# Channel mixer of layer 1 over all tokens at once, in seven block products instead of eight

## The chip, the cores and the metric

The kernel runs on one core of a Trainium2 chip. The metric is the device time of one execution in microseconds. TensorE (PE) multiplies, VectorE (DVE) and GpSimd (POOL) do elementwise work, ScalarE (ACT) casts and activations, SyncE (SP) issues the transfers between DRAM and the core's memory (SBUF). Products are accumulated in PSUM.

## What is computed

A trunk of two layers over 1024 tokens of width 1024. Each layer has a token mixer (RWKV in the first, sparse attention, DSA, in the second) and a channel mixer; shift, scale and gate of each come from a projection of a conditioning vector. The channel mixer has a hidden width of 2816:

```python
def _swiglu(h, w_in, w_out):
    gate, up = jnp.split(h @ w_in, 2, axis=-1)
    return (jax.nn.silu(gate) * up) @ w_out
...
        x = _layernorm(DEEPNORM_ALPHA * x + (1 + gt1) * y, ln_g[i, 0], ln_b[i, 0])
        hin = x * (1 + sc2) + sh2
        y = _swiglu(hin, ffn_w_in[i], ffn_w_out[i])
        x = _layernorm(DEEPNORM_ALPHA * x + (1 + gt2) * y, ln_g[i, 1], ln_b[i, 1])
```

## The kernel before

Every large product is made of three products of rounded parts: each operand is split into a high part (`whi`, a cast on ACT, L204) and a low part (`wlo`, the difference, on DVE or POOL in a rota kept in `low`, L121), and `mm3` (L232 to 235) multiplies high by high, high by low and low by high. One matmul is 128 rows of weights by 512 columns, `128x512` in the profile.

`ffn(0, (0, 1), zt, rest, x=x)` is the channel mixer of the first layer. It takes the tokens in two halves of 512. For each half and each of 22 column blocks `j` of 128, `gate_up` makes the gate (24 matmuls) and the up product (24 matmuls), the silu, the product of the two (L1171, DVE) and its high and low parts (`hid`). The down product follows after groups of 8, 7 and 7 blocks (`FG`), and `evac_y` (L812, L813) adds it into the residual rows `R`. Those were scaled by the previous LayerNorm's gain and bias in `resid` (L806, L807, on POOL, 128x1024). At the end come the LayerNorms (`layernorm`, L818 to L832), which write `z` back to DRAM (L829).

Other work is threaded into it. The tail of the token mixer runs step by step from the generator `bg`, four steps for each call of `rest`; its last parts are two output pairs of 48 matmuls (`psg<-whi,oq`), their LayerNorm and the write of the second half's rows. `ada_v(1, ·)` makes twelve columns of the next layer's modulation: four loads of 512 KB, eight operations on DVE (L305, L307) and four small matmuls (L310) each. `hin_prep` transposes `z` (L886) and makes the next hidden input with its parts (L890 to L892), for the second half of this mixer and for the next layer while PE goes on with products. The engines take their instructions in the order in which a scheduler placed them; a load goes out on SP when its buffer is free. Weights come through three buffers `wst` of 128x1024, the modulation through buffers `z` of a pool `big`.

## Time and profile before

| | before |
|---|---|
| median of 3 runs | 3320.2 us (3309.88 to 3321.77) |
| the profiled execution | 3313.66 us, span 3311.9 us, mean granted clock 0.958 |
| PE busy, share of the span | 3066.4 us, 93% |
| DVE | 2154.5 us, 65% |
| ACT | 1351.4 us, 41% |
| POOL | 993.9 us, 30% |
| DRAM traffic | 438.42 MB, mean 132 GB/s |
| the stage of this mixer | 1018.9 to 1809.8 us |

Busy shares are of the whole span, and stages differ; the views of the next but one section are therefore cut to the stage. A busy PE is one with a matmul in flight: the pipelined matmuls overlap, so the time from one to the next, and not the duration of one, is its price. The granted clock (PEclk) is 1.00 at 2.4 GHz and 0.50 at 1.2 GHz.

### The profile page before, as it was taken

The page shows a single profiled execution, that of the slowest core. Times are in us where ns is not written, and L with a number is a line of the kernel's source. Part 1 is how long each engine was busy: PE and PEld are TensorE (multiplying, and loading weights), DVE is VectorE, ACT ScalarE, POOL GpSimd, SP SyncE. Part 2 cuts the span into 40 slices and gives each one's busy share as a digit, 9 for nine tenths or more (in the row PEclk, how much of TensorE's full clock was granted, in tenths as well). Part 3 has the DMA queues.
Part 4 walks back from the last instruction along what each step waited for, and adds up shares of the span by engine and source line. Part 5 has one row for each costly group of instructions (what it writes and reads, how often), then busy time and mean ns, then how long its engine had stood idle before and what let it go on. Part 6 is the DMA issues. An engine that isn't in the chain of part 4 may idle for free. (4 is left out here: it accounts for less than half of the span.)

```text
span 3311.9 us, 48942 instructions
## 1 busy us (share of the span) xinstructions
PE 3066.4 (93%) x17888; PEld 2414.2 (73%) x17888; DVE 2154.5 (65%) x4239; ACT 1351.4 (41%) x2512; POOL 993.9 (30%) x780
## 2 busy tenths in 40 slices
PE   6889689989989999999999999988999999899998
PEld 2466257688777788877888776677887777687886
DVE  4576578756766764583334577786697788775345
ACT  3552344234444222232223745646622466452223
POOL 3261135201112411251112122556222432443112
PEclk8989888999999999999999999998999999999999
DMA  6556756598874653463332622244323411253333
GB/s 195 145 167 175 131 173 171 138 180 156 187 171 123 229 188 115 154 224 102 93 99 94 186 83 73 65 132 139 96 90 111 143 63 34 91 167 101 92 99 121
DMA packets 611057, 438.42 MB, mean 132 GB/s; under 512 B 207936, under 2 KB 508480, under 8 KB 610816
## 3 DMA queue, kind: packets, MB, share of 16 engines
q1 hardware_dynamic: 610816, 435.29, 47.0%
q8 instruction: 141, 2.31, 0.3%
q14 instruction: 100, 0.82, 0.1%
HBM read 379.12 MB, written 55.95 MB: 131 GB/s over the span
## 5 line engine op out<-in xcount | busy, mean ns | idle before, releaser
L204 ACT CAST whi<-wst 128x512 fp32r<-128x512 f32 x886 | 541.4, 619 | 1262.0 <-PE psu L234 569.7
L121 POOL TENSOR_TENSOR wlo<-wst,whi 128x512 fp32r<-128x512 f32 x330 | 460.7, 1397 | 1508.8 <-ACT whi L204 1474.8
L121 DVE TENSOR_TENSOR wlo<-wst,whi 128x512 fp32r<-128x512 f32 (+1 forms) x556 | 470.8, 851 | 504.2 <-ACT whi L204 498.7
L233 PE MATMUL psu<-hin,whi 128*128 128x512 f32 (+1 forms) x1568 | 587.5, 375 | 39.2 <-DVE sl L1171 22.4
L234 PE MATMUL psu<-hin,whi 128*128 128x512 f32 (+1 forms) x1568 | 586.6, 374 | 8.4 <-DVE hin L907 3.3
L235 PE MATMUL psu<-hin,wlo 128*128 128x512 f32 (+1 forms) x1568 | 584.5, 373 | 0.1
L233 PEld LDWEIGHTS psu<-hin,whi 128*128 128x128 f32 x1568 | 301.9, 193 | 93.7 <-DVE sl L1171 25.6
L234 PEld LDWEIGHTS psu<-hin,whi 128*128 128x128 f32 x1568 | 302.6, 193 | 60.2 <-DVE hin L907 6.1
L235 PEld LDWEIGHTS psu<-hin,wlo 128*128 128x128 f32 x1568 | 302.1, 193 | 50.6 <-POOL wlo L121 0.6
L234 PE MATMUL psg<-wlo,hid 128*128 128x512 f32 x528 | 206.4, 391 | 0.0
L233 PE MATMUL psg<-whi,hid 128*128 128x512 f32 x528 | 205.2, 391 | 0.0
L235 PE MATMUL psg<-whi,hid 128*128 128x512 f32 x528 | 205.1, 389 | 0.0
L233 PE MATMUL psg<-xs,whi 128*128 128x512 f32 x384 | 164.1, 436 | 19.8 <-ACT whi L204 11.0
L234 PE MATMUL psg<-xs,whi 128*128 128x512 f32 x384 | 164.9, 430 | 8.4 <-POOL xs L121 5.7
L235 PE MATMUL psg<-xs,wlo 128*128 128x512 f32 x384 | 161.2, 421 | 1.7 <-DVE wlo L121 1.7
L1171 DVE TENSOR_TENSOR sl<-sl,psu 128x512 f32<-128x512 f32 (+1 forms) x98 | 61.7, 630 | 148.3 <-PE psu L235 138.2
L233 PEld LDWEIGHTS psg<-xs,whi 128*128 128x128 f32 x384 | 77.8, 204 | 52.5 <-ACT whi L204 13.0
L233 PEld LDWEIGHTS psg<-whi,hid 128*128 128x128 f32 x528 | 99.1, 188 | 20.9
L235 PEld LDWEIGHTS psg<-whi,hid 128*128 128x128 f32 x528 | 99.1, 188 | 20.8
L234 PEld LDWEIGHTS psg<-wlo,hid 128*128 128x128 f32 x528 | 99.2, 188 | 20.8 <-DVE wlo L121 0.6
L115 ACT ACTIVATE z<-z,mx 128x128 f32<-128x128 f32 (+7 forms) x128 | 99.2, 776 | 32.6 <-DVE mx L1529 31.6
L234 PEld LDWEIGHTS psg<-xs,whi 128*128 128x128 f32 x384 | 77.2, 201 | 38.3 <-issue 9.7
(418 smaller groups left out, 6472.2 us busy)
## 6 DMA issues: line engine op xcount, KB each, us to landing
wst<-in_ffn_w_in_dram SPq DMA_DIRECT2D x196, 512.0 KB
wst<-in_ffn_w_out_dram SPq DMA_DIRECT2D x92, 512.0 KB
wst<-in_rwkv_w_rkv_dram SPq DMA_DIRECT2D x48, 512.0 KB
z<-in_ada_w_dram SPq DMA_DIRECT2D x48, 512.0 KB
wst<-in_ada_w_dram SPq DMA_DIRECT2D x32, 512.0 KB
wst<-in_rwkv_w_out_dram SPq DMA_DIRECT2D x64, 256.0 KB
wst<-in_dsa_w_out_dram SPq DMA_DIRECT2D x32, 512.0 KB
wst<-in_dsa_w_in_dram SPq DMA_DIRECT2D x26, 512.0 KB
```

The source lines that it names most:

```text
L115: return A.activation(o, i, f, **kw)
L121: i = eng.tensor_tensor(lo, x, hi.bitcast(F32), op=OP.subtract)
L204: A.copy(h_[:, :m], st[:, c:c + m])
L233: mm(o, lh, rh, start=first, stop=False)
L234: mm(o, lh, rl, start=False, stop=False)
L235: mm(o, ll, rh, start=False, stop=last)
L1171: V.tensor_tensor(sl[:, c], sl[:, c], ou[:, c], op=OP.mult)
```

## The change

`ffn` is no longer used for this mixer; `ffn_both(0, x)` takes its place. Tokens, inner width and outer width are each cut in two, and both products are made of seven block products instead of eight, after Strassen and Winograd: sums and differences of the blocks of the operands are multiplied, and the results are added to each other.

- **Up.** For each column block `j` seven products of 12 matmuls (`prod`), with four combinations of the four weight blocks (`b11`, `b12`, `b21`, `b22`; half the inner width, gate or up) on DVE and POOL. The combinations of the hidden input (`s2`, `s3`, `s1`, `a22`, `s4`, high and low, 40 tiles) are made once, from `z` read back from DRAM through `wst` and transposed (L1311 of the changed kernel). They need both halves of the tokens; so the products of four blocks (`NP = 4`) with the first half alone are made ahead, under the tail of the token mixer, and kept in the `R` buffers. The results are joined by additions from PSUM on DVE, silu and product follow (`gmul`, POOL), and of each pair of blocks `j` and `j + 11` the hidden blocks and their combinations, seven in all, go to `hd` in DRAM.
- **Down.** The 22 blocks of the down weights are loaded whole, 44 loads of 256 KB, and stay; their memory is that of the combinations of the hidden input. Each product reads its seven times 11 hidden blocks back from `hd` through `wst` and splits them (cast on ACT, low on DVE); the combinations of the weights `t1` to `t4` are made on DVE and POOL, and all lows of weights are POOL's. The residual rows are scaled by DVE and POOL in turn, four rows each.
- **Moved.** `ada_v` uses `wst` instead of `big`, two columns each at `jj = 2` and `4` and one each at the even `jj` from 6 to 20. The pool `big` is opened after the mixer, three small factor tiles are freed ahead of it. The hidden input of the mixer's second half is no longer made by `hin_prep`, and that of the next layer comes after the last product.

The program of PE has 15025 instructions before and 14661 after, 396 matmuls of 128x512 fewer and 32 transposes more.

```diff
+    fp_ = pool(sf, "fac")
...
     sc0.close()
+    sf.close()
     sb.close()
...
-                bp.append(pool(ctx, "big", side="right"))
...
-    ffn(0, (0, 1), zt, rest, x=x)
+    def prod(o, w, c, xh, xl, first):
+        (h_,), (l_,) = w
+        for k in range(4):
...
+            mm(o, h_[:, s], xh[k][:, c], start=first and k == 0, stop=False, **kw_)
+            mm(o, h_[:, s], xl[k][:, c], start=False, stop=False, **kw_)
+            mm(o, l_[:, s], xh[k][:, c], start=False, stop=k == 3, **kw_)
...
+    def ffn_both(l, x):
...
+        hd = tc.dram_tile([7, FP, P, HN], F32, name=f"hd{l}")
...
+            ws2 = lambda: f.tile([P, 1024], F32, tag="ws2", bufs=2, name="ws2")
...
+            def wload(t, off):
+                dma(t.rearrange("p (k n) -> p k n", n=P), dap(win, bi + off, [[2 * FH, P], [P * 2 * FH, KT], [1, P]]))
+                return t[:, 0:HN], t[:, HN:2 * HN]
...
+            (a11h, a12h), (a11l, a12l) = ((t[0:4], t[4:8]) for t in x)
...
+            for j in range(0, NP, 2):
...
+                for i in range(2):
+                    b11, b21 = wload(wst(), (j + i) * P)
+                    kept.append(rtile())
...
+                    prod(o[i], split(b11, HN), full, a11h, a11l, True)
+                    A.copy(kept[-1][:, 0:HN], o[i])
+                    rest(None)
+                for i in range(2):
+                    prod(o[i], split(b2[i], HN), full, a12h, a12l, False)
+                    act(kept[j + i][:, HN:2 * HN], o[i], AF.Silu)
+                    rest(None)
+            while bg:
+                rest(None)
+            with ExitStack() as sc_:
...
+                for nm in ("s2", "s3", "s1", "a22", "s4"):
+                    com[nm] = [[cpool.tile([P, HN], F32R, name=f"{nm}{hl}{i}") for i in range(4)] for hl in "hl"]
+                for i in range(4):
...
+                    for m in range(2):
+                        zb = wst()
+                        for e in range(2):
+                            dma(zb[:, e * HN:e * HN + HN].rearrange("p (a n) -> p a n", n=P),
+                                dap(zd[2 * l][m], (i + 4 * e) * P, [[D, P], [P * D, NTT], [1, P]]))
+                        for e in range(2):
+                            pt = pst()
+                            for b in range(NTT):
+                                nc.tensor.transpose(pt[:, b * P:b * P + P], zb[:, e * HN + b * P:e * HN + b * P + P], ident)
...
+                            act(r_, pt, scale=hsc[:, 2 * l + 1, ft:ft + 1], bias=hbi[:, 2 * l + 1, ft:ft + 1])
+                            raw[m, e] = r_
+                    s1, s2 = hf32(), hf32()
+                    tt(V, s1, raw[1, 0], raw[1, 1], add_)
+                    tt(V, s2, s1, raw[0, 0], sub_)
+                    tt(G, raw[0, 0], raw[0, 0], raw[1, 0], sub_)
+                    tt(V, raw[0, 1], raw[0, 1], s2, sub_)
+                    for n_, (nm, r_) in enumerate((("s2", s2), ("s3", raw[0, 0]), ("s1", s1), ("a22", raw[1, 1]), ("s4", raw[0, 1]))):
...
+                        A.copy(hi_, r_)
+                        sub(G if n_ in (1, 3) else V, lo_, r_, hi_)
...
+                for jj in range(FT):
+                    j = jj // 2 + FP * (jj % 2)
+                    b11, b21 = wload(wst(), j * P)
+                    b12, b22 = wload(ws2(), FH + j * P)
+                    early = j < NP
+                    if early:
+                        u2, sl0 = kept[j][:, 0:HN], kept[j][:, HN:2 * HN]
+                    else:
+                        u2, sl0 = tl("u2", 2), tl("sl0")
+                        oa = psx("u")
+                        prod(oa, split(b11, HN), full, a11h, a11l, True)
+                        A.copy(u2, oa)
+                    tt(V, b11, b12, b11, sub_)
...
+                    tt(V, t2, b22, b11, sub_)
...
+                    prod(ob, split(t2, HN), full, *com["s2"], True)
+                    if not early:
+                        prod(oa, split(b21, HN), full, a12h, a12l, False)
+                        act(sl0, oa, AF.Silu)
+                    tt(V, u2, ob, u2, add_)
+                    tt(G, b12, b22, b12, sub_)
...
+                    prod(oc, split(b12, HN), full, *com["s3"], True)
...
+                    tt(V, u3, oc, u2, add_)
...
+                    prod(od, split(b11, HN), full, *com["s1"], True)
+                    tt(G, b21, b21, t2, sub_)
+                    prod(oc, split(b21, HN), full, *com["a22"], False)
+                    tt(V, u3, od, u3, add_)
...
+                    tt(V, sl1, oc, u2, add_)
+                    act(sl1, sl1, AF.Silu)
...
+                    gmul(h1, u3, sl1)
+                    prod(od, split(b22, HN), full, *com["s4"], False)
+                    tt(V, u2, od, u2, add_)
...
+                    gmul(h0, u2, sl0)
+                    hids[j] = h0, h1
+                    if j >= FP:
+                        (a21, a11), (a22, a12) = hids.pop(j - FP), hids.pop(j)
+                        k = j - FP
+                        for q, t in ((0, a11), (1, a12), (2, a22)):
+                            dma(hd[q, k], t)
+                        s1, s2 = hf32(), hf32()
+                        tt(G, s1, a21, a22, add_)
+                        dma(hd[3, k], s1)
+                        tt(G, s2, s1, a11, sub_)
+                        dma(hd[4, k], s2)
+                        s4 = hf32()
+                        tt(V, s4, a12, s2, sub_)
+                        dma(hd[6, k], s4)
+                        s3 = hf32()
+                        tt(V, s3, a11, a21, sub_)
+                        dma(hd[5, k], s3)
+                    elif l == 0 and nada[0] < 12 and j >= 1:
+                        for _ in range(2 if nada[0] < 4 else 1):
+                            ada_v(1, nada[0], wst, hf32)
+                            nada[0] += 1
...
+            w = [wq.tile([P, D], F32, name=f"wo{k}") for k in range(FT)]
+            for k, n in [(k, 0) for k in range(FT)] + [(k + h * FP, 1) for k in range(FP) for h in (1, 0)]:
+                dma(w[k][:, n * HN:n * HN + HN], dap(wo, bo_ + k * P * D + n * HN, [[D, P], [1, HN]]))
...
+            lg = tp.tile([P, D], F32, name="lg")
+            rmore = [tp.tile([P, D], F32, name=f"Rm{i}") for i in range(NTT)]
...
+            dma(g_, dap(modd[l], (24 + 16) * P, [[0, P], [1, D]]))
...
+            dma(lg, dap(a["ln_g"], i * D, [[0, P], [1, D]]))
+            dma(lbs, dap(a["ln_b"], i * D, [[0, P], [1, D]]))
+            V.tensor_scalar(lg, lg, ALPHA, None, op0=OP.mult)
+            V.tensor_scalar(lbs, lbs, ALPHA, None, op0=OP.mult)
+            rr = [[rtile() for _ in range(NTT)], rmore]
+            for m in (1, 0):
+                for t_ in range(NTT):
+                    r = rr[m][t_]
+                    dma(r, zd[i][m][t_ * P:t_ * P + P, :])
+                    (G if t_ % 2 else V).tensor_tensor(r, r, lg, op=OP.mult)
+                    (G if t_ % 2 else V).tensor_tensor(r, r, lbs, op=OP.add)
+            def t1(k):
+                tt(V, left(k), right(k), left(k), sub_)
+            def t2(k):
+                t1(k)
+                t = f32()
+                tt(G, t, right(k + FP), left(k), sub_)
+                return t
+            def t3(k):
+                tt(G, right(k), right(k + FP), right(k), sub_)
+                return right(k)
+            def t4(k):
+                t = f32()
+                tt(V, t, left(k + FP), right(k + FP), sub_)
+                tt(G, t, t, left(k), add_)
+                return t
+            def product(q, wk, o, first):
+                for k in range(FP):
+                    if k % 2 == 0:
+                        nk = min(2, FP - k)
+                        st_ = wst()
+                        dma(st_[:, :nk * HN].rearrange("p (k n) -> p k n", n=HN), hd[q, k:k + nk].rearrange("k p n -> p k n"))
+                    raw = st_[:, k % 2 * HN:k % 2 * HN + HN]
+                    xh, xl = hint(), hint()
+                    A.copy(xh, raw)
+                    sub(low[0], xl, raw, xh)
...
+                    (wh,), (wl,) = split(wk(k), HN)
+                    for b in range(NTT):
...
+            def out(m, n, o, u):
+                for b in range(NTT):
+                    t = hf32()
...
+                    if u is None:
+                        V.scalar_tensor_tensor(t, gn, 1.0, o[b], op0=OP.add, op1=OP.mult)
+                    else:
+                        tt(V, u[b], o[b], u[b], add_)
+                        V.scalar_tensor_tensor(t, gn, 1.0, u[b], op0=OP.add, op1=OP.mult)
+                    r = rr[m][b][:, n * HN:n * HN + HN]
+                    tt(G, r, r, t, add_)
+            oa, ob = quad(), [psu(), psu(), pst(), pst()]
+            product(0, left, oa, True)
...
+            for b in range(NTT):
+                A.copy(u2[b], oa[b])
+            product(4, t2, ob, True)
+            for b in range(NTT):
+                tt(V, u2[b], ob[b], u2[b], add_)
+            product(1, lambda k: left(k + FP), oa, False)
+            out(1, 0, oa, None)
+            product(5, t3, ob, True)
...
+            for b in range(NTT):
+                tt(V, u3[b], ob[b], u2[b], add_)
+            product(3, left, oa, True)
+            out(0, 1, oa, u3)
+            product(2, t4, ob, False)
+            for b in range(NTT):
+                t = hf32()
+                tt(V, t, ob[b], u2[b], add_)
+                V.scalar_tensor_tensor(t, g_[:, 0:HN], 1.0, t, op0=OP.add, op1=OP.mult)
+                r = rr[0][b][:, 0:HN]
+                tt(V, r, r, t, add_)
+                layernorm(l, 1, 0, b, rr[0][b], tp)
+            product(6, lambda k: right(k + FP), oa, False)
+            out(1, 1, oa, u2)
+            for b in range(NTT):
+                layernorm(l, 1, 1, b, rr[1][b], tp)
+        low[:] = [V, V, G]
+    NP = 4
+    ffn_both(0, x)
+    bp.append(pool(ctx, "big", side="right"))
```

Three places in the order of the instructions, with the names of the programs (a number behind a name tells buffers apart). The first is the end of the token mixer's tail on PE. Before, up products follow the last output pair to the end of the half:

```order
L233 MATMUL psg<-whi,oq 128x512
L234 MATMUL psg<-wlo,oq 128x512
L235 MATMUL psg<-whi,oq 128x512
L233 MATMUL psu<-hin,whi 128x512
L234 MATMUL psu<-hin,whi 128x512
L235 MATMUL psu<-hin,wlo 128x512
```

After, 57 matmuls of the early blocks follow it, and then this; `pst<-cst,wst` are the transposes of the hidden input, `s2`, `s3` its combinations:

```order
L1250 MATMUL psu<-hin,whi 128x512
L1251 MATMUL psu<-hin,whi 128x512
L1252 MATMUL psu<-hin,wlo 128x512
L1311 MATMUL pst<-cst,wst 128x128 x56
L1250 MATMUL psu<-s2h_10271,whi 128x512
L1251 MATMUL psu<-s2l_10275,whi 128x512
L1250 MATMUL psg<-s3h_10279,whi 128x512
L1251 MATMUL psg<-s3l_10283,whi 128x512
L1252 MATMUL psu<-s2h_10271,wlo 128x512
```

Behind the early products stand 56 transposes in one run, and the next product takes a combination of both halves.

The second is a modulation column on DVE. Before, its eight operations (L305, L307) lie among the lows of weights and the gate products of two blocks:

```order
L1171 TENSOR_TENSOR sl<-sl,psu 128x512
L121 TENSOR_TENSOR wlo<-wst,whi 128x512
L311 TENSOR_TENSOR modf<-pst,vf 128x4
L125 TENSOR_SCALAR hid<-sl 128x512
L305 TENSOR_SCALAR yt<-z_12508,csr 128x512
L121 TENSOR_TENSOR hid<-sl,hid 128x512
L307 SCALAR_TENSOR_TENSOR yt<-z_12508,csr,yt 128x512
L307 SCALAR_TENSOR_TENSOR yt<-z_12512,csr,yt 128x512 x2
L307 SCALAR_TENSOR_TENSOR yt<-z_12516,csr,yt 128x512 x2
L121 TENSOR_TENSOR wlo<-wst,whi 128x512
L307 SCALAR_TENSOR_TENSOR yt<-z_12520,csr,yt 128x512 x2
```

After, at `jj = 2`; `hf` is the accumulator, `L1266` the combinations and additions:

```order
L1266 TENSOR_TENSOR sl_10851<-psg,R 128x512
L307 SCALAR_TENSOR_TENSOR hf_10875<-wst,csr,hf_10875 128x512 x3
L1266 TENSOR_TENSOR R<-psg,R 128x512
L307 SCALAR_TENSOR_TENSOR hf_10875<-wst,csr,hf_10875 128x512 x4
L305 TENSOR_SCALAR hf_10898<-wst,csr 128x512
L307 SCALAR_TENSOR_TENSOR hf_10898<-wst,csr,hf_10898 128x512
L311 TENSOR_TENSOR modf<-pst,vf 128x4
L307 SCALAR_TENSOR_TENSOR hf_10898<-wst,csr,hf_10898 128x512 x6
L1266 TENSOR_TENSOR wst<-ws_11079,wst 128x512
L1266 TENSOR_TENSOR wst<-ws_10923,wst 128x512
L311 TENSOR_TENSOR modf<-pst,vf 128x4
L1266 TENSOR_TENSOR t_10946<-ws_10923,wst 128x512
```

The operations of two columns now stand in two long runs, and the combinations of the next block's weights (`wst<-ws,wst`) behind them.

The third is the scaling of the residual rows. Before, on POOL (L806, L807), between lows of weights:

```order
L121 TENSOR_TENSOR wlo<-wst,whi 128x512
L806 TENSOR_TENSOR R<-R,z_13713 128x1024 x2
L807 TENSOR_TENSOR R<-R,z_13714 128x1024
L121 TENSOR_TENSOR wlo<-wst,whi 128x512
L807 TENSOR_TENSOR R<-R,z_13714 128x1024
L806 TENSOR_TENSOR R<-R,z_13713 128x1024
L121 TENSOR_TENSOR wlo<-wst,whi 128x512
L807 TENSOR_TENSOR R<-R,z_13714 128x1024
L806 TENSOR_TENSOR R<-R,z_13713 128x1024
L807 TENSOR_TENSOR R<-R,z_13714 128x1024
```

After, on POOL between product 0 and product 4 of the down product; `L1266` with `hin` makes `t2`, `L121` its low part:

```order
L1266 TENSOR_TENSOR wo_13935<-wo_13946,wo_13935 128x512
L1417 TENSOR_TENSOR R<-R,lg 128x1024 x2
L1417 TENSOR_TENSOR Rm_13993<-Rm_13993,lg 128x1024
L1418 TENSOR_TENSOR R<-R,wst 128x1024 x2
L1417 TENSOR_TENSOR Rm_13995<-Rm_13995,lg 128x1024
L1418 TENSOR_TENSOR Rm_13993<-Rm_13993,wst 128x1024
L1266 TENSOR_TENSOR hin<-wo_13936,wo_13925 128x512
L1266 TENSOR_TENSOR hin<-wo_13937,wo_13926 128x512
L1266 TENSOR_TENSOR hin<-wo_13938,wo_13927 128x512
L1266 TENSOR_TENSOR hin<-wo_13939,wo_13928 128x512
L1418 TENSOR_TENSOR Rm_13995<-Rm_13995,wst 128x1024
L121 TENSOR_TENSOR wlo<-hin,whi 128x512 x4
```

The eight rows' scaling, of which POOL and DVE have half each, stands ahead of the combinations of the second product's weights. On SP the transfers that it needs stand behind the loads of all down weights:

```order
L1398 DMA wo_13934<-in_ffn_w_out_dram 128x512
L1398 DMA wo_13946<-in_ffn_w_out_dram 128x512
L1398 DMA wo_13935<-in_ffn_w_out_dram 128x512
L1408 DMA lg<-in_ln_g_dram 128x1024
L1416 DMA Rm_13992<-z_1_91 128x1024
L1416 DMA Rm_13993<-z_1_91 128x1024
L1416 DMA Rm_13994<-z_1_91 128x1024
L1416 DMA Rm_13995<-z_1_91 128x1024
L1444 DMA wst<-hd_9754 128x2x512 x5
```

The gain `lg`, the rows `Rm` and the first hidden blocks of that product follow the last of the 44 loads of weights.

## Rows read from the trace of the kernel before

**Rows 1.** Stretches of core 0, by window (us busy, with instructions in brackets).

```profile
core 0: us, PE busy (x) PEld busy (x) DVE busy (x) ACT busy (x) POOL busy (x), PEclk, DMA share, GB/s
...
1100.00:1137.00 37.00, 31.77 (x135) 25.85 (x134) 34.17 (x34) 7.71 (x13) 20.12 (x9) 0.91 0.89 308
...
1400.00:1500.00 100.00, 94.00 (x412) 76.97 (x411) 79.12 (x106) 30.66 (x46) 49.50 (x29) 0.95 0.63 208
1500.00:1600.00 100.00, 100.00 (x449) 82.80 (x448) 38.69 (x57) 24.89 (x41) 15.49 (x12) 1.00 0.30 94
...
1700.00:1809.80 109.80, 109.80 (x494) 91.08 (x493) 43.40 (x66) 30.53 (x52) 22.80 (x17) 1.00 0.31 93
1018.90:1809.80 790.90, 775.89 (x3469) 639.40 (x3469) 434.05 (x620) 222.16 (x363) 205.04 (x135) 0.99 0.45 142
```

**Rows 2.** Timeline of PE in the loop: start us, us, what.

```profile
1734.66 0.39 PE L233 MATMUL psu<-hin,whi 128*128 128x512 f32 x1
...
1747.36 0.39 PE L235 MATMUL psu<-hin,wlo 128*128 128x512 f32 x1
```

**Rows 3.** Timeline of PE after the wait near 1478 us.

```profile
1479.28 0.63 PE L234 MATMUL psu<-hin,whi 128*128 128x512 f32 x1
1479.70 0.63 PE L235 MATMUL psu<-hin,wlo 128*128 128x512 f32 x1
```

**Rows 4.** Waits of PE from 1100 to 1500 us: total, times, longest.

```profile
PE psu L233 <- DVE sl L1171: 11.2, 3, 5.2
```

**Rows 5.** Timeline of POOL from 1116 us.

```profile
1119.83 11.11 POOL L806 TENSOR_TENSOR R<-R,z 128x1024 f32<-128x1024 f32 x4 [5.26 <-DVE z L790]
```

**Rows 6.** Timeline of DVE in the same stretch.

```profile
1118.40 0.75 DVE L307 SCALAR_TENSOR_TENSOR yt<-z,csr,yt 128x512 f32<-128x512 f32 x1
...
1119.67 0.69 DVE L121 TENSOR_TENSOR wlo<-wst,whi 128x512 fp32r<-128x512 f32 x1
1120.27 2.89 DVE L307 SCALAR_TENSOR_TENSOR yt<-z,csr,yt 128x512 f32<-128x512 f32 x1
...
1131.41 0.67 DVE L1171 TENSOR_TENSOR sl<-sl,psu 128x512 f32<-128x512 f32 x1
```

**Rows 7.** Groups of instructions, 1137 to 1809 us: busy us, mean ns of one.

```profile
L121 DVE TENSOR_TENSOR wlo<-wst,whi 128x512 fp32r<-128x512 f32 x158 | 126.8, 804 | 225.4 <-ACT whi L204 223.3 <-PE psu L234 2.0
...
L121 POOL TENSOR_TENSOR wlo<-wst,whi 128x512 fp32r<-128x512 f32 x79 | 109.9, 1392 | 473.5 <-ACT whi L204 468.6 <-DMA R<-z 4.9
...
L307 DVE SCALAR_TENSOR_TENSOR yt<-z,csr,yt 128x512 f32<-128x512 f32 x70 | 65.4, 958 | 0.4
...
L807 POOL TENSOR_TENSOR R<-R,z 128x1024 f32<-128x1024 f32 x7 | 19.4, 2788 | 2.2 <-PE psu L234 2.1
...
L818 DVE BATCH_NORM_STATS2 st<-R 128x6 f32<-128x512 f32 x10 | 6.7, 682 | 0.0
...
L115 ACT ACTIVATE R<-R,mv 128x1024 f32<-128x1024 f32 x4 | 4.8, 1239 | 1.1 <-DVE mv L823 1.1
```

**Rows 8.** Timeline of POOL from 1054 us, an operation alone.

```profile
1058.25 1.30 POOL L121 TENSOR_TENSOR wlo<-wst,whi 128x512 fp32r<-128x512 f32 x1 [4.46 <-ACT whi L204]
```

**Rows 9.** Timeline of DVE at the end of the tail's second output pair.

```profile
1086.92 0.68 DVE L812 SCALAR_TENSOR_TENSOR yt<-G,psg 128x512 f32<-128x512 f32 x1
```

**Rows 10.** Timeline of SP, the write of that pair's rows.

```profile
1096.63 0.71 SPq L829 DMA_DIRECT2D z<-R  x1
```

**Rows 11.** Waits of all engines, 1137 to 1809 us: total, times, longest.

```profile
POOL wlo L121 <- DMA R<-z: 4.9, 1, 4.9
```

**Rows 12.** Transfers from 1010 to 1200 us, in 40 slices.

```profile
GB/s 231 216 0 13 46 107 110 88 159 99 167 172 184 133 109 170 182 201 284 379 352 392 357 350 317 188 40 12 332 211 110 79 45 131 81 110 110 110 114 35
```

**Rows 13.** Timeline of PE where the next layer's hidden input is transposed.

```profile
1900.48 1.03 PE L886 MATMUL pst<-cst,z 128*128 128x128 f32 x8
1902.29 0.91 PE L233 MATMUL psg<-hin,whi 128*72 128x512 f32 x3 [0.77 <-ACT hin L115]
```

63 lines of the change are left out of this document (60 added, 3 removed).

## The prediction

> **What bounds the kernel now.** I read the table of stretches first, then the timelines of PE, POOL and DVE where PE stops, then the groups of instructions. The stage that changes runs from 1018.9 to 1809.8 us, 790.9 us, and PE is busy for 775.9 us of it; from 1500 us on it never stops, at a granted clock of 1.00 [rows 1]. Matmuls of 128x512 follow each other every (1747.36 - 1734.66) / 56 = 0.227 us there [rows 2]. So TensorE's instruction count is the price of this stage, and whatever takes matmuls away is paid back in full, as long as the other engines keep up. Twice they don't: PE waits 11.2 us in all, 5.2 us at the longest, for the gate product on VectorE [rows 4]. The reason stands beside it. While POOL works through residual rows of 1024, at 11.11 / 4 = 2.78 us each [rows 5], a DVE operation with two SBUF inputs that takes 0.69 or 0.75 us takes 2.89 us, and one with an input in PSUM takes its usual 0.67 us [rows 6]. DVE and POOL take turns when each has two inputs in SBUF. After each of the two spells the clock is at its lower level for some microseconds: 0.91 over 37 us and 0.95 over 100 us, or 3.3 and 5.0 us lost [rows 1], with 0.42 us from matmul to matmul meanwhile [rows 3].
>
> **What the change removes.** Up: 22 column blocks x 7 products x 12 matmuls = 1848 instead of 2112. Down: 7 products x 11 x 12 = 924 instead of 1056. That is 396 fewer, 396 x 0.227 = 89.8 us [rows 2]. It adds 32 transposes, since both halves of the hidden input are transposed again and before only one was: 32 x 1.03 / 8 = 4.1 us [rows 13]. With the clock losses of before taken off, PE's work is 775.9 - 8.3 - 89.8 + 4.1 = 682 us. **The break-even is 790.9 - 682 = 109 us**: if PE loses more than this to waiting and to a lower clock, the kernel is slower. Before lost 23 us. The rest of the working is the list of what it will lose.
>
> **Start: 34 us (20 to 45).** Before, the first half's gate and up products go on under the tail of the token mixer. Now only 96 matmuls of four column blocks may go ahead; 57 of them (13 us) stand behind the last output pair, and then come 56 transposes and products that need the combinations of both halves. Of the second output pair, the end on DVE (1086.92 us) and the write of its rows (1096.63) lie 9.7 us apart [rows 9, 10]; write and read back have no row of their own, so I take 4.9 us each, the wait for such a reload [rows 11] (from 1.4 us, half a megabyte at 379 GB/s [rows 12]). That is 19.5 us. Each of the four combinations then holds six DVE operations and three POOL operations with two SBUF inputs, 6 x 0.69 + 3 x 1.30 = 8.0 us in turns [rows 6, 8], and the first product needs the last one's s2: 28 us. Less 13 us of matmuls and 7 us of transposes: 28, plus 6 for the gaps that the tail has anyway. Without turns and with quick reloads it is 20.
>
> **Loop: 34 us (15 to 58).** A pair of column blocks gives PE 168 matmuls, 38.1 us. POOL has 17 operations of 512 for it (7 lows of weights, 4 combinations, 4 gate products, s1, s2), DVE 13 with two SBUF inputs, and where a column of the next layer's modulation is made, 8 more. Clean prices give 17 x 1.30 + 13 x 0.69 + 8 x 0.75 = 37.1 us if they take turns [rows 6, 8]: 97% of PE's time, where before the stage had 205 us of POOL in 791 [rows 1]. The additions that read PSUM don't count. Two pairs, those of blocks jj = 2 and 4, carry two modulation columns each and one early block: 16 x 1.30 + 12 x 0.69 + 16 x 0.75 = 41.1 us against 12 x 12 matmuls, 32.6 us. There the order puts sixteen operations in a row on DVE ahead of the next block's weights, and the eight loads they need share three buffers with those weights. I take 11 us for each of the two, and 1.5 us for each of the eight pairs with one column. The upper end takes the mean prices of the stage, 1.39, 0.80 and 0.96 us [rows 7], which hold the waits already seen: 41.7 us for a pair with one column, 47.2 us for one with two, so 8 x 3.6 + 2 x 14.6 = 58; the lower end is 2 x 8.5 less a little lookahead. [...]
>
> **Between up and down: 10 us (8 to 13).** The first load of the down weights stands on SP behind the last sums' writes to DRAM, which wait for a DVE addition, a gate product and two sums on POOL and two on DVE: 0.67 + 3 x 1.30 + 2 x 0.69 = 6 us. A load (1.4 to 4.9 us, as above), a cast and a low follow. The low can be late by one matmul only.
>
> **Second product of down: 33 us (18 to 45).** On SP, 44 loads of 256 KB, 11.5 MB, stand ahead of the LayerNorm gain, the second half's rows and the second product's sums. At 350 to 390 GB/s, the best that before shows [rows 12], they take 31 us; the gain lands some 41 us after the last up matmul, when product 0 (132 matmuls, 29.9 us) is just ending at 10 + 30. The scaling of the rows then takes seven operations of 1024 on POOL and as many on DVE, ahead of the sums and lows of weights that the second product needs, POOL at about 2.78 us apiece [rows 7] and DVE in its gaps: 24 us. Then four sums and the first low. The second product begins near 67 us, goes by POOL's two operations and one DVE operation per block, 11 x 3.3 = 36 us, and ends near 105 instead of 70; taking off 2 us of overlap, 33. Without turns it is 18; with rows a little later still, 45. Products 1, 5, 3 and 6 have one POOL operation per block and stay PE's. Product 2 has two POOL and two DVE per block: 44 us against 29.9, most of it made ahead: 4 us (0 to 14).
>
> **End: 13 us (4 to 18).** At 1809.8 the next layer's products follow without a gap [rows 1], because their hidden input was prepared under the last group. Now its activations stand on ACT behind the LayerNorm of the second half, which needs product 6: eight DVE operations, then eight statistics at 0.68 us [rows 7, 9], small ones, and 1.24 us on ACT [rows 7]: about 15 us, less what ACT gets in early.
>
> **Clock: 10 us (3 to 17).** PE now stands still for long at five places. A spell of 5.2 us was followed by a loss of 3.3 us [rows 1, 4]; the second product goes by POOL and does not care.
>
> **Sum.** 34 + 34 + 10 + 33 + 4 + 13 + 10 = 138 us lost against 109: 29 us slower. On the profiled execution's own 3313.7 us (span 3311.9) that is 3343. The median of the three runs, 3320.2, is 6.5 us higher and the lowest run lower; I keep 3343.
>
> **Rivals.** That the change doesn't do what it says is ruled out: the order counts 396 matmuls fewer. (1) *DVE and POOL keep clear of each other*, because six buffers of highs and lows let POOL run a block ahead: all terms at their lower ends, 20 + 15 + 8 + 18 + 0 + 4 + 3 = 68, 41 us faster, 3273. For it: with POOL busy for a quarter of the stage before [rows 1], the lows came in time; PE waited only beside operations of 1024. It decides as soon as the losses stay under 109 us. Chance 0.25. (2) *Only the fixed places cost*: start 30, loop 15, 10, 28, 0, 8 and 5 = 96, 13 us faster, 3301 to 3320, no difference that can be told. Chance 0.20. (3) *The loop is bound by the two engines in turns*, all prices at the mean of the stage and the other terms high: 45 + 58 + 13 + 45 + 14 + 18 + 17 = 210, 101 us slower, 3415; from 3380 on. Chance 0.13. My forecast, 3325 to 3370, has 0.42.
>
> **How the numbers follow.** A measurement of this kernel tells about 0.5%, 17 us, from no change: 3304 to 3337. Faster: rival 1 and a quarter of rival 2, 0.30. Same: the rest of rival 2 and the lower part of the forecast, 0.26. Slower: 0.44. The range takes the middle of rival 1 to the start of rival 3, 3272 to 3392, and leaves out about a fifth.
>
> **What would show it.** Right: a PE gap of 25 us or more before the first product with s2; stops of 10 us and more at the two double columns; PE idle between the first and second product of down while POOL does rows of 1024; a gap before the next layer's projections. POOL and DVE busy over 90% together in the loop. Wrong: PE at 1.00 through the loop with stops under 1 us, or rows of 1024 done before the gain was needed.

## The result, and the profile after

The changed kernel takes 3444.0 us (median of 4 runs, 3442.7 to 3448.3) against 3321.0 us before: ratio 1.038, interval 1.0355 to 1.0405. It is 123 us slower. The forecast was 3343, 23 us above the median of 3320.2 that it stood beside, within 3272 to 3392. The direction came out as forecast; the size did not, and the time lies outside the range. The profiled execution took 3442.8 us, its span 3440.7.

The page of the changed kernel, busy time of each engine and the slices of PE, POOL and PE's granted clock:

```profile
PE 3057.9 (89%) x17524; PEld 2376.2 (69%) x17524; DVE 2265.8 (66%) x4246; ACT 1402.5 (41%) x2610; POOL 1314.7 (38%) x1000
...
PE   7889789889887779998498899988899999899998
...
POOL 3251244111123545554877321555422432434112
PEclk8988889989997889999699999999999999999999
```

PE executes 396 matmuls less and 32 transposes more, and yet it is busy for 3057.9 us, where it was 3066.4 before: most of what it saved in instructions it gave back, at a lower clock above all. The 20th slice shows the worst place at a glance: PE at 4 tenths, POOL at 8, clock at 6.

The same by stretch (columns as in [rows 1]). The stage now runs from 1018.9 to 1926.5 us, 907.6 us against 790.9:

```profile
core 0: us, PE busy (x) PEld busy (x) DVE busy (x) ACT busy (x) POOL busy (x), PEclk, DMA share, GB/s
1018.90:1120.00 101.10, 72.16 (x296) 53.55 (x295) 62.16 (x80) 47.45 (x79) 41.98 (x31) 0.81 0.40 117
...
1160.00:1252.00 92.00, 65.98 (x260) 52.09 (x258) 55.49 (x75) 13.19 (x24) 37.72 (x26) 0.81 0.54 177
...
1160.00:1631.00 471.00, 416.66 (x1715) 331.80 (x1713) 262.08 (x347) 111.25 (x192) 238.75 (x164) 0.92 0.44 143
1297.00:1610.00 313.00, 294.69 (x1233) 235.03 (x1231) 168.99 (x228) 81.09 (x141) 170.93 (x119) 0.96 0.42 134
1675.00:1715.00 40.00, 2.39 (x6) 1.25 (x5) 36.41 (x15) 5.62 (x11) 40.00 (x18) 0.54 0.26 91
1018.90:1926.50 907.60, 746.94 (x3074) 590.40 (x3072) 543.21 (x637) 269.54 (x456) 529.62 (x354) 0.89 0.43 137
```

Before, the clock stood at 0.99 over the stage [rows 1]; now at 0.89. The two levels are 1.2 and 2.4 GHz, so a mean of 0.89 means the lower one for (1 - 0.89) / 0.5 = 22% of the time, some 200 us. POOL is busy for 529.6 us where it was for 205.0. Between the two profiled executions the span grew by 128.8 us: 116.7 in this stage, the other 12 behind it.

**Where the time went.** I added up the distances from one matmul's start to the next where they are over 0.5 us, less the 0.227 us of a matmul at full pace. They hold the slow first matmul behind each stop; without it, PE's idle time in the stage is 907.6 - 746.9 = 161 us, of which the loop has 58. The clock and the pace are from the shorter distances. Beside it stands what the prediction gave each term:

| term (us) | forecast | measured |
|---|---|---|
| PE's work at full pace | 682 | 682 (not measured by itself) |
| start, 1018.9 to 1120 | 34 | 32 |
| loop, 1120 to 1631 | 34 | 65 |
| between up and down | 10 | 12 |
| second product of down | 33 | 39 |
| other products of down | 4 | 13 |
| end | 13 | 14 |
| lower clock | 10 | about 40 |
| slower pace at full clock | 0 | about 10 |
| sum | 820 | 907, of 907.6 |

The clock's 40 us are an estimate: 162 matmuls at a distance of 0.38 to 0.5 us lost 31 us, and PE was busy for 101 us at the lower clock, half of which would be 50. Four terms hold within 6 us: start, between up and down, second product, end. The loop, the clock, the pace and the small products make up the error.

**The loop.** PE's waits and the waits of those that feed it, 1160 to 1631 us (us in total, times, longest):

```profile
PE pst L310 <- DVE hf L307: 31.7, 5, 6.5
PE psu L1250 <- ACT whi L204: 18.0, 8, 3.2
...
ACT whi L204 <- DMA wst<-in_ffn_w_in_dram: 53.4, 10, 17.2
DVE hf L1266 <- DMA hd<-hf: 32.5, 9, 4.8
```

```profile
SPq L1273 <- DVE hf L307: 25.9, 19, 1.7
```

Five waits are for the modulation column (`hf`, L307), eight for the first high of a block's weights. Behind the latter stands a late load into `wst`; DVE itself stood still for 32.5 us for writes to `hd` to land; and SP waited 25.9 us with loads of weights (L1273) for DVE to be done with the columns (L307). One pair of blocks shows the chain, in the order of time (timeline of all engines):

```profile
1415.38 0.69 DVE L1266 TENSOR_TENSOR hf<-hid,hf 128x512 f32<-128x512 f32 x1 [4.76 <-DMA hd<-hf]
...
1418.19 0.49 DVE L305 TENSOR_SCALAR hf<-wst,csr 128x512 f32<-128x512 f32 x1 [0.79 <-DMA hd<-hf]
...
1421.54 1.94 SPq L1273 DMA_DIRECT2D wst<-in_ffn_w_in_dram  x2
...
1426.14 0.62 ACT L204 CAST whi<-wst 128x512 fp32r<-128x512 f32 x1 [1.73 <-DMA wst<-in_ffn_w_in_dram]
...
1426.82 0.50 PE L1250 MATMUL psu<-hin,whi 128*128 128x512 f32 x1 [2.77 <-ACT whi L204]
```

`hf32` has two buffers, and they hold the sums until their writes to DRAM have landed. DVE wants to make s4 and stands 4.76 us; then the modulation column wants the same tiles and waits again. Its source tiles are three buffers of `wst`, which come free only as DVE works through them; so SP issues the load of the next block's weights at 1421.54, the cast waits for it, and PE stands 2.8 us.

Where two columns stand in a row, PE waits twice:

```profile
1182.22 1.84 PE L310 MATMUL pst<-ones,hf 128*128 128x1 f32 x8 [6.10 <-DVE hf L307]
1190.50 1.83 PE L310 MATMUL pst<-ones,hf 128*128 128x1 f32 x8 [6.45 <-DVE hf L307]
```

Those are 12.5 us, and 12.8 for the second double column (1229 to 1244). During the first of these stops DVE is at work on the column (L307) almost without a break, from 1175.9 to 1182 us; during the second it waits 1.4 us for a column's load. The fifth of these waits, 6.3 us at 1289.82, is that of the first single column. Each stop costs a second time. After the stop at 1332.9, PE's own rows:

```profile
1332.46 0.40 PE L1252 MATMUL psg<-s4h,wlo 128*128 128x512 f32 x1
1335.75 0.50 PE L1250 MATMUL psu<-hin,whi 128*128 128x512 f32 x1 [2.89 <-ACT whi L204]
...
1338.13 0.63 PE L1250 MATMUL psu<-hin,whi 128*128 128x512 f32 x1
1338.56 0.63 PE L1251 MATMUL psu<-hin,whi 128*128 128x512 f32 x1
```

From 1338 to 1343 us matmuls follow each other at 0.43 us instead of 0.23. Such a stretch, 2.6 to 5.1 us long, stands behind each of the six stops of 2.4 to 3.2 us for first highs.

**Between products 0 and 4.** POOL, DVE, ACT and PE after 1675 us:

```profile
1680.66 6.61 POOL L1417 TENSOR_TENSOR R<-R,lg 128x1024 f32<-128x1024 f32 x2
1687.23 3.31 POOL L1417 TENSOR_TENSOR Rm<-Rm,lg 128x1024 f32<-128x1024 f32 x1
...
1703.63 7.26 POOL L1266 TENSOR_TENSOR hin<-wo,wo 128x512 f32<-128x512 f32 x4
```

```profile
1685.00 3.35 DVE L1417 TENSOR_TENSOR Rm<-Rm,lg 128x1024 f32<-128x1024 f32 x1
```

```profile
1705.36 0.62 ACT L204 CAST whi<-hin 128x512 fp32r<-128x512 f32 x1 [21.35 <-POOL hin L1266]
```

```profile
1706.04 1.22 PE L1454 MATMUL psu<-whi,hin 128*128 128x512 f32 x2 [30.81 <-ACT whi L204]
...
1714.91 0.80 PE L1455 MATMUL psu<-wlo,hin 128*128 128x512 f32 x1 [6.80 <-POOL wlo L121]
```

Seven operations of 1024 on POOL from 1680.66 to 1703.63, 3.3 us each, while DVE's of the same size take 3.35: the two in turns, as in [rows 5, 6]. The sums of weights (`hin<-wo,wo`) that the second product needs stand behind them, the cast behind the sums, PE behind the cast. That is the 33 us of the prediction, where it said and by the scaling of the rows that it named; e6 and e8 try how much of it hangs on the loads and how much on the two engines.

### The profile page after: what moved, and what is told of

The parts are those of the page before. It is cut to its first block, busy times and chain, and to the rows that moved or that the text cites. A ratio compares the mean times of both kernels' runs of the same rounds, so it can differ in the third digit from the quotient of the medians.

```text
span 3440.7 us, 48730 instructions
## 1 busy us (share of the span) xinstructions
PE 3057.9 (89%) x17524; PEld 2376.2 (69%) x17524; DVE 2265.8 (66%) x4246; ACT 1402.5 (41%) x2610; POOL 1314.7 (38%) x1000
## 5 line engine op out<-in xcount | busy, mean ns | idle before, releaser
L121 POOL TENSOR_TENSOR wlo<-wst,whi 128x512 fp32r<-128x512 f32 x293 | 408.6, 1396 | 1089.0 <-ACT whi L204 1052.6
L204 ACT CAST whi<-wst 128x512 fp32r<-128x512 f32 (+1 forms) x710 | 429.8, 617 | 847.7 <-PE psu L234 260.4
L121 DVE TENSOR_TENSOR wlo<-wst,whi 128x512 fp32r<-128x512 f32 x417 | 372.0, 898 | 312.8 <-ACT whi L204 305.6
L233 PE MATMUL psu<-hin,whi 128*128 128x512 f32 (+1 forms) x864 | 308.0, 357 | 27.3 <-ACT sl L115 15.3
L234 PE MATMUL psu<-hin,whi 128*128 128x512 f32 (+1 forms) x864 | 307.9, 356 | 7.9 <-DVE hin L909 3.3
L235 PE MATMUL psu<-hin,wlo 128*128 128x512 f32 (+1 forms) x864 | 306.5, 355 | 0.2 <-POOL wlo L121 0.2
L233 PEld LDWEIGHTS psu<-hin,whi 128*128 128x128 f32 x864 | 166.4, 193 | 53.2 <-ACT sl L115 16.9
L234 PEld LDWEIGHTS psu<-hin,whi 128*128 128x128 f32 x864 | 167.3, 194 | 30.6 <-DVE hin L909 6.1
L235 PEld LDWEIGHTS psu<-hin,wlo 128*128 128x128 f32 x864 | 167.4, 194 | 22.4 <-POOL wlo L121 0.6
L121 DVE TENSOR_TENSOR hin<-wst,hin 128x512 fp32r<-128x512 f32 x77 | 89.4, 1175 | 75.9 <-ACT hin L1447 55.7
L234 PE MATMUL psg<-wlo,hid 128*128 128x512 f32 x264 | 103.5, 392 | 0.6 <-DVE wlo L121 0.6
L235 PE MATMUL psg<-whi,hid 128*128 128x512 f32 x264 | 102.3, 389 | 0.0
L233 PE MATMUL psg<-whi,hid 128*128 128x512 f32 x264 | 102.0, 390 | 0.0
L121 POOL TENSOR_TENSOR wlo<-wo,whi 128x512 fp32r<-128x512 f32 x55 | 80.5, 1478 | 42.3 <-ACT whi L204 42.1
```

The lines of the kernel that those rows point to most:

```text
L121: i = eng.tensor_tensor(lo, x, hi.bitcast(F32), op=OP.subtract)
L204: A.copy(h_[:, :m], st[:, c:c + m])
L233: mm(o, lh, rh, start=first, stop=False)
L234: mm(o, lh, rl, start=False, stop=False)
L235: mm(o, ll, rh, start=False, stop=last)
```

## The experiments

All run beside the kernel before on the same chip, which then took 3313 to 3316 us in the median.

**e1: the sums without `hf32`.** s1 and s2 go into tiles of other names, s3 in place; only s4 uses `hf32`.

```diff
-                        s1, s2 = hf32(), hf32()
+                        s1, s2 = tl("u3"), tl("sl1")
...
-                        s3 = hf32()
-                        tt(V, s3, a11, a21, sub_)
-                        dma(hd[5, k], s3)
+                        tt(V, a21, a11, a21, sub_)
+                        dma(hd[5, k], a21)
```

> The four sums of hidden blocks (s1 to s4) no longer take turns in the two hf32 buffers that the modulation columns accumulate in: s1 and s2 go into tiles that are free at that time, s3 into a21. The theory of the buffers (DVE stands still until a sum has landed in DRAM, 32.5 us in the loop, the modulation operations behind it come late, give their staging buffers back late, and so the next block's weights come late): DVE's wait for hd falls from 32.5 us to under 5, PE's gap of 2.4 to 3.2 us per pair falls under 1 us and the lower clock behind it goes; 30 to 45 us faster than the changed kernel (3444), about 3405. The rival (DVE and POOL in turns): the operations are the same, so within 5 us of 3444.

Measured: 3411.2 us, 33 us less than the changed kernel, ratio to before 1.030 (1.024 to 1.036); by the two ratios it is 27 us. PE's wait for columns and DVE's for landing writes, 1160 to 1600 us:

```profile
PE pst L310 <- DVE hf L307: 23.6, 4, 9.3
```

```profile
DVE u L1266 <- DMA hd<-u: 1.1, 2, 0.5
```

DVE's 32.5 us of waiting for landing writes are down to 1.1, and PE's 18.0 us of waiting for first highs to 2.8; the four stops of the two double columns stay (3.1 + 9.3 and 3.2 + 8.0 us). So the buffers that are held until a write lands cause the stops at single columns, and not those at double ones.

**e2: the modulation columns out of `wst`.** They are loaded into the `R` buffers, which lie idle once the early products are used, one column per block from `jj = 8` on. The place and the time change at once, and no two columns stand in a row any more; the place and the time take the columns' loads off the weights' way.

```diff
-                    elif l == 0 and nada[0] < 12 and j >= 1:
-                        for _ in range(2 if nada[0] < 4 else 1):
-                            ada_v(1, nada[0], wst, hf32)
-                            nada[0] += 1
+                    if l == 0 and nada[0] < 12 and jj >= 8:
+                        ada_v(1, nada[0], rtile, hf32)
+                        nada[0] += 1
```

> The twelve modulation columns are staged through the R buffers, which are free then, instead of the weights' wst, and made one per block from jj = 8 to 19 instead of two at jj = 2 and 4 and one at the even blocks to 20. The theory of the staging (the columns' loads hold the three buffers that the next block's weights need): the gaps of 6 us in four places (25 us) and the 2.4 to 3.2 us per pair go, with 15 to 20 us of lower clock; 50 to 65 us faster than the changed kernel, 3380 to 3395. The rival (DVE and POOL in turns): what a pair has to do is as much as before from jj = 8 on and more by 8 operations of 0.75 us, over PE's 38.1 us, so a pair keeps taking 44 us or more there, and only the four early gaps go: 3415 or more.

Measured: 3368.2 us, 76 us less (70 by the ratios); ratio 1.017 (1.011 to 1.023). The loop by stretch, and DVE's wait for landing writes, 1160 to 1600 us:

```profile
1160.00:1563.80 403.80, 395.70 (x1714) 317.22 (x1712) 289.09 (x348) 111.12 (x192) 242.35 (x164) 0.98 0.52 166
```

```profile
DVE hf L1266 <- DMA hd<-hf: 12.4, 10, 4.8
```

The loop from 1160 us to its end takes 403.8 us instead of 471, at a clock of 0.98; PE has no gap over 2 us. DVE still waits 12.4 us for landing writes, and no stop of PE over 2 us comes of it. 67 of the 76 us lie in the loop, its clock loss included. DVE and POOL have as many operations there as in the changed kernel (348 on DVE and 164 on POOL; there 347 and 164) and are busy no less (289.1 + 242.4 us against 262.1 + 238.8), so it is not fewer turns that freed the loop. What this run does not separate is what bound the double columns: the buffers shared with the weights, or the run of sixteen operations on DVE.

**e3: e1 and e2 together.** 

> e1_sums and e2_ada together, nothing else. e9_all (with the down phase on DVE, worth 32 us, and the 32 bytes) came to 3351, where e2_ada alone less 32 would be 3336; a pair of blocks takes 44.5 us there against 42.0 in e2_ada. If e1_sums' edit costs once the modulation columns have buffers of their own (s1 and s2 hold tiles that the next block needs until they are written): 3378 to 3386, slower than e2_ada's 3368. If its gain adds: 3350. If the 32 bytes or the down phase cost it: 3365 to 3370.

Measured: 3381.4 us, ratio 1.020 (1.017 to 1.023): by its ratio some 11 us above e2 alone, though the intervals overlap. A pair of blocks takes 44.6 us, in e2 42.0. Once the columns have buffers of their own, e1's edit gains nothing and seems to cost. The cause given ahead of the run, that `u3` and `sl1` are held until a write lands and the next block needs them, does not show: in this trace DVE waits for no write to `hd`. What PE waits for, 1160 to 1600 us, is the column once more, 7.1 us in nine stops where it is 2.9 in three in e2:

```profile
PE pst L310 <- DVE hf L307: 7.1, 9, 1.3
```

Why the columns come later on DVE stays open.

**e5: no turns in the loop.** All of POOL's work from the first block of the loop to the last goes to DVE.

```diff
+                low[:] = [V]
...
-                    tt(G, b12, b22, b12, sub_)
+                    tt(V, b12, b22, b12, sub_)
...
-                    gmul(h1, u3, sl1)
+                    tt(V, h1, u3, sl1, OP.mult)
...
-                        tt(G, s1, a21, a22, add_)
+                        tt(V, s1, a21, a22, add_)
```

(and likewise the other operations on POOL there.)

> In the loop of the up products every elementwise operation of POOL (lows of weights, two combinations of weights, gate products, sums s1 and s2) is DVE's; the rest is the changed kernel. A pair with one modulation column then holds 30 operations of 0.69 us, 8 of 0.75 and 10 additions from PSUM of 0.69 on DVE alone, 33.6 us, instead of 37.1 us of DVE and POOL in turns beside 7 us of additions. If turns bound the loop: the gaps per pair shrink, 25 to 40 us faster than the changed kernel's 3444. If the staging of weights and the sums' buffers bound it, as the runs with other buffers say: DVE's row of instructions gets longer and what waits for a landing write holds back more, so no gain or a loss, 3440 to 3470.

Measured: 3446.3 us, no change; ratio 1.039 (1.035 to 1.044). The loop by stretch:

```profile
1160.00:1633.50 473.50, 415.91 (x1685) 329.91 (x1683) 317.22 (x505) 110.52 (x191) 0.00 (x0) 0.91 0.44 139
```

POOL does nothing, and PE is busy for 415.9 us as it was (416.7 in the changed kernel). DVE takes 317.2 us in place of DVE's 262.1 and POOL's 238.8 together. What stood in the way in the changed kernel still stands there, 1160 to 1600 us:

```profile
DVE hf L1266 <- DMA hd<-hf: 30.3, 11, 4.9
```

```profile
PE psu L1250 <- ACT whi L204: 28.2, 12, 5.2
```

By itself the run leaves open that DVE's longer row cost what the missing turns gained. With e2, where the turns stayed and the loop lost 67 us, it follows that turns of DVE and POOL, by which the prediction had priced the loop, were not what bound it. This is the step that failed.

**e4: 32 bytes of padding.** A tile of 32 bytes is added ahead of the other buffers.

```diff
+    cp.tile([P, 8], F32, name="pad")
```

> A tile of 32 bytes is added ahead of the weights' buffers, nothing else. In the trace of the changed kernel the products with the combinations (s1 to s4, a22) take 0.233 us from matmul to matmul instead of 0.227, and so do products ahead of the stage that nothing in the change touches (psg<-xs,whi: 0.2285 before, 0.233 after). Between the kernels the weights' buffers moved by 1056 bytes, an odd multiple of 32. If the distance of the two operands' addresses decides, the pace of both goes back (0.227 and 0.2285), and the kernel is 8 to 15 us faster, about 3432. If something else decides (the load on DVE, the accumulator), nothing changes: 3444.

Measured: 3445.2 us, no change in time; but the pace of matmuls at full clock changes. In the changed kernel twelve matmuls with s1, then the same in e4:

```profile
1415.31 0.39 PE L1250 MATMUL psg<-s1h,whi 128*128 128x512 f32 x1
...
1417.87 0.40 PE L1252 MATMUL psg<-s1h,wlo 128*128 128x512 f32 x1
```

```profile
1419.38 0.39 PE L1251 MATMUL psg<-s1h,whi 128*128 128x512 f32 x1
...
1421.89 0.40 PE L1253 MATMUL psg<-s1h,wlo 128*128 128x512 f32 x1
```

Eleven distances: 2.56 / 11 = 0.233 us against 2.51 / 11 = 0.228; over some 1240 matmuls with combinations the means are 0.2336 and 0.2296. Products with `xs` before the stage show it too (0.233, with padding 0.229, before the change 0.229). Which operand's address decides, or whether it is their distance, no run shows. In the stage that should be worth 1240 x 0.004 = 5 us; the time does not show them.

**e6: residual rows earlier.** The gain and the rows are loaded after 11 of the 44 loads of down weights instead of behind all.

```diff
+            wload_([(k, 0) for k in range(FP)])
...
                     dma(r, zd[i][m][t_ * P:t_ * P + P, :])
...
+            wload_([(k, 0) for k in range(FP, FT)] + [(k + h * FP, 1) for k in range(FP) for h in (1, 0)])
```

> The LayerNorm gain and the residual rows are loaded after the first 11 of the 44 loads of down weights instead of after all, so their scaling can run during the first product of down. The theory of the order (33 us in the prediction): the gap of 30.8 + 6.8 us between the first and the second product falls under 12 us, 25 to 35 us faster than the changed kernel, about 3414. The rival (POOL and DVE in turns are the bound of both products): the first product is stretched by what the gap loses, and at most 10 us are won.

Measured: 3446.1 us, no change; ratio 1.040 (1.033 to 1.048). The gap ahead of the second product is 20.9 + 2.6 us instead of 30.8 + 6.8, but product 0 takes 44.3 us instead of 32.2:

```profile
1655.60:1699.90 44.30, 37.24 (x132) 29.52 (x132) 36.00 (x16) 8.66 (x16) 42.09 (x20) 0.82 0.90 330
```

POOL is busy for 42.1 of these 44.3 us, with rows and lows of product 0, and behind them it makes ten sums for a later product (16.7 us from 1702.11) ahead of those for the second. The wait only moved. The queue of loads, on which the prediction's 33 us partly rested, is not the cause; POOL's and DVE's work is.

**e8: e6, and all of POOL's work of down on DVE.**

```diff
+            low[:] = [V]
...
-                    (G if t_ % 2 else V).tensor_tensor(r, r, lg, op=OP.mult)
+                    V.tensor_tensor(r, r, lg, op=OP.mult)
...
-                tt(G, right(k), right(k + FP), right(k), sub_)
+                tt(V, right(k), right(k + FP), right(k), sub_)
```

> As e6_rr (gain and residual rows loaded after 11 of the 44 loads), and in the down phase every elementwise operation of POOL is DVE's. By turns, the seven products of the changed kernel hold about 270 us of both engines (154 lows, 55 combinations of weights, 16 scalings, 32 additions of the results) against 210 us of PE, and 268 us is what the phase took; on DVE alone the same operations are 170 to 185 us. If turns bound it: from the first down product to the last the phase falls from 266 us (e6_rr) to 225 to 240, 3405 to 3420 in all. If DVE as such is the bound: 266 us or longer, 3446 or more.

Measured: 3413.6 us, 32 us less than e6; ratio 1.029 (1.026 to 1.033). From the first matmul of down to the first stop at its end it takes 240.7 us against 268.1. DVE's rows:

```profile
1657.26 1.22 DVE L1421 TENSOR_TENSOR Rm<-Rm,lg 128x1024 f32<-128x1024 f32 x1
1658.39 1.22 DVE L1422 TENSOR_TENSOR R<-R,wst 128x1024 f32<-128x1024 f32 x1
```

Alone, DVE does a row of 1024 every 1.13 us. With POOL beside it the two did two such rows in 3.3 us. One engine is faster than two, as it must be if they exclude each other and POOL is the slower. The Trainium skill (SBUF — State Buffer, "Who interferes with whom") says that a VectorE instruction with two SBUF inputs and a GpSimd instruction that reads SBUF share a port which one of them holds at a time; the trace agrees.

**e9: e1, e2, the padding and e8 together; e10: e9 and e5's edit.**

> e1_sums, e2_ada, e4_pad and e8_downV together. e2_ada brought 76 us and e1_sums 33, which overlap where both shorten the same gaps; the down phase as in e8_downV, 30 us. If the gains add: 3444 - 80 - 30 = 3334. The start (30 us), the step from up to down (12 us) and the end (12 us) stay. If down does not gain: 3365.

> e9_all with e5_upV's loop: no operation of POOL in either loop. With the waits for buffers gone, the pairs that carry two modulation columns hold 37.1 + 6 us in turns, more than PE's 38.1; on DVE alone 39.6. If turns are what is left in the loop (42 us per pair in e2_ada): 10 us faster than e9_all. If DVE alone is worse: slower by up to 20 us.

Measured: e9 3350.6 us, ratio 1.010 (1.007 to 1.014), 17 us above what the gains would add up to; e10 3318.9 us (8 runs), ratio 1.001 (0.9998 to 1.0023). The edit that did nothing by itself (e5) is worth 32 us here. A pair of blocks takes 44.5 us in e9 and 40.4 in e10. The loop of e10 by stretch:

```profile
1160.00:1540.80 380.80, 380.75 (x1707) 312.63 (x1705) 308.01 (x510) 113.97 (x192) 0.00 (x0) 1.00 0.54 175
```

PE never stops, at full clock, as before the change from 1500 us on [rows 1]. The loop ends 28.6 us earlier than in e9 (1540.8 against 1569.4). So POOL's share of the work was the second limit of the loop, hidden behind the first. Whether by the turns or because POOL's own operations are the slower ones (1.30 us in [rows 8] against 0.69 in [rows 6]) the runs do not separate.

**e11, e12, e13: what is left in e10.** e11 gives the raw tiles of the combinations a second set and puts the scaling of the rows, and the sums `t3`, behind the second product's lows. e12 is e11 with the next layer's hidden input asked for ahead of the second half's LayerNorm. e13 is e12 without the second set, and makes the products of block `j = 11` with the first half ahead as well. The line of each that matters:

```diff
+                    alt = [ws2(), ws2()] if i % 2 else None
...
+            product(4, t2, ob, True)
+            mark = lastv[0]
+            scale(1)
```

```diff
+                    dma(w[t_], zd[1][0][t_ * P:t_ * P + P, :])
+                pre.append(hin_prep(2, 0, w[0:NTT]))
```

```diff
+            b11, b21 = wload(wst(), FP * P)
+            k11 = tl("u2", 2), tl("sl0")
```

> e10_allV with two more edits. The combinations of the hidden input take their four raw tiles from two sets in turn instead of one (each of the four rounds took 8.7 us, since ACT's next activations wait for the raw tiles): 7 to 10 us less at the start. And in the down phase the scaling of the residual rows and the combinations for the fourth product are issued after the lows of the second product instead of ahead of them: the gap of 12.4 + 2.7 us between first and second product falls under 4 us, about 10 us. If both are on the path: 17 us faster than e10_allV, 3300 to 3303, 0.4% faster than before. If DVE's row is only pushed back, the stall comes back at the third or fourth product and 3310 to 3315 is left.

> e11_late, and the next layer's hidden input of the first half is made from down weights' tiles that are free by then, ahead of the LayerNorms of the second half instead of behind them. In e10_allV PE idles some 10 us between the last down product and the next layer's projections. If the order on ACT behind the LayerNorms is the cause, 4 to 8 us of it go: about 3296. If the reload of the rows or the buffers of the hidden input hold it, nothing: as e11_late.

> e12_end without the second set of raw tiles (which moved the wait of the start to its end: 14.3 us in one piece), and the first block of the second half, j = 11, has its products with the first half of the tokens made ahead of the combinations too (24 matmuls, 5.4 us that need no combination). If the start is on the path and PE has nothing else to do there: 7 + 5 us less than e12_end, 3309. If its casts and lows delay the combinations by as much, 3314: then what the start costs is set by LayerNorm, reload and combinations, and not by what PE could do meanwhile.

Measured: ratios to before 1.002 (1.001 to 1.003), 1.003 (1.001 to 1.004) and 1.001 (0.999 to 1.002): 3321.2, 3321.0 and 3316.1 us. None gains a measurable amount over the kernel before. In e11 the start's waits become one long one, and in e12 PE still waits at the end:

```profile
1133.59 0.79 PE L1251 MATMUL psu<-s2h,whi 128*128 128x512 f32 x1 [14.34 <-ACT whi L204]
```

```profile
1789.56 0.44 PE L889 MATMUL pst<-cst,wo 128*128 128x128 f32 x2 [1.67 <-DMA wo<-z]
1795.16 0.69 PE L889 MATMUL pst<-cst,wo 128*128 128x128 f32 x2 [5.17 <-DMA wo<-z]
1799.54 0.69 PE L889 MATMUL pst<-cst,wo 128*128 128x128 f32 x2 [3.70 <-DMA wo<-z]
```

In e11 the transposes are done early, and the first product with s2 still waits for the combinations: the start is the time that these take. The gap ahead of the second product falls there from 12.4 to 7.6 us, but product 1, under which the rows are scaled now, takes 33.5 us instead of 29.7. At the end PE waits for the first half's rows of `z`, on their way through DRAM, in e12 as in the changed kernel.

## Why the prediction was wrong in size

*What bounds the kernel, PE's work and the break-even: right.* The stage's sum closes with 682 us of work (907 of 907.6, within the clock's estimate). Losses were 226 us, not 138, against a break-even of 109.

*Start, 34 us: right in size, not in shape, and so in part by luck.* 32 us, but not one wait of 25 us ahead of the first product with s2: four rounds of transposes with gaps of 1.7 to 2.8 us, since the four sets of raw tiles are not there at once. e11, with more tiles, shows the one wait.

*Loop, 34 us: the step that failed.* It measured 65. I priced it by DVE and POOL in turns and asked how far the sum goes over PE's time. Two things were wrong. First, turns were not the limit (e2: turns kept, 67 us gained; e5: turns gone, no change). The limit was a chain of buffers, visible in the code and in the change: `hf32` has two, four sums per pair pass through them, and each is held until its write has landed; the columns use the same two; and the columns' loads share three `wst` with the weights. I used this last point for the double columns, 11 us each, and they measured 12.5 and 12.8. For the eight singles I took 1.5 us each from a sum of busy times; PE stood 6.3 us at the first, 2.4 to 3.2 at the next six and 1.2 at the last. A busy sum does not contain waits for landing, and 4.76 us of them stood in front of the columns. Second, I expected "POOL and DVE busy over 90% together in the loop" as a sign; they are, (169.0 + 170.9) / 313 = 109%, and it told nothing: above 100% they did not always exclude each other, and e5 took POOL away without effect. POOL's share of the work does limit, at about 4 us per pair (e9 to e10), once the buffers do not.

*Between up and down, 10 us: right* (11.7).

*Second product of down, 33 us: right in the main* (30.8 + 6.8), by DVE and POOL in turns on rows of 1024 (e8). The part of the argument on the order of loads does not carry it (e6).

*Other products, 4 us: too small*, 13, of which product 2 has 6.5 (2.5 + 4.0), within its range.

*End, 13 us: right in size by luck, wrong in mechanism.* PE's rows there in the changed kernel:

```profile
1917.77 0.69 PE L888 MATMUL pst<-cst,z 128*128 128x128 f32 x2 [5.10 <-DMA z<-z]
1922.00 0.69 PE L888 MATMUL pst<-cst,z 128*128 128x128 f32 x2 [3.54 <-DMA z<-z]
1926.45 0.69 PE L888 MATMUL pst<-cst,z 128*128 128x128 f32 x2 [3.77 <-DMA z<-z]
```

It waits for the reload of the first half's `z`, not for ACT behind the LayerNorm of the second half.

*Clock, 10 us: mis-sized, about 40.* I took one loss per long stop at five places. The lower clock also follows the stops of 3 us, and 24 stops lasted 2.4 us or more. In e10, with the loop's stops gone, about half of that time at the lower clock is left. A stop cost more than the time it lasted; the term should have been tied to the number of stops.

*Pace, not in the sum:* about 10 us, of which 5 are the padding's.

*The rivals.* Rival 3 (3415, from 3380 on) is where the time fell, and past it. But its mechanism, turns in the loop, was not the cause. The error is above all in the loop's and the clock's terms: about 30 us each, of the 88 us by which the losses exceeded the sum.

**What stays open.** In e13 the next layer's first product begins at 1797.0 us, 13 us earlier than before, and the run is not faster: from that product to the end the profiled execution takes 1518 us, where it takes 1502 before (after the change 1513, in e2 1509, in e10 1511). The code there is the same; I found no cause. The kernel before was profiled once, and its own times here spread over 13 us (3307.4 to 3320.8), so part of it may be that. Nor is it known why matmuls with `hin` in the loop run at 0.230 us and not 0.227 with or without the padding.

## What to carry to other kernels

A scheme that trades matmuls for additions must be priced by its buffers first: for each added tile that goes to DRAM, ask how many buffers it cycles through, how long it is held until its write has landed, and what stands behind the waiting instruction; sums of busy time do not show it. Removing one limit shows the next (e5 alone nothing, on top of e9 32 us), so an experiment that does nothing is repeated once the first limit is gone. And the 90 us of saved matmuls were just about eaten by what could not be hidden: the start, the step from up to down, the first rows of down and the end, with all limits of the loop removed.

## What the runs showed of the hardware that I had not expected

- Matmuls of 128x512 at full clock follow each other at 0.233 or 0.229 us depending on where their operands lie: 32 bytes of padding, nothing else, changed it (e4).
- Moving two-input work from POOL to DVE, with no engine added, is worth 27 us in down (240.7 against 268.1 us) and 32 us from e9 to e10, 28.6 of them by the end of the loop: POOL does not help DVE there, it hinders it.
- It is not only operations with two inputs in SBUF that POOL holds up: before the change a DVE operation on 128x1024 with one SBUF input took 2.88 us beside POOL's rows (L791 at 1123.09 us), its like just ahead of them 0.69 (L790 at 1119.07).
- A stop of 2.4 to 3.2 us in the loop is followed by 2.6 to 5.1 us in which matmuls take 0.43 us apiece; at the longest such stretch the stop costs nearly twice what it lasts (2.9 us, and 5.1 x (1 - 0.23 / 0.43) = 2.4 us), at the others 1.2 to 1.6 us more.
